# One Trainium2 core, a hybrid encoder block: DMA scratch of 64 bytes, and the first two w_up jobs prepared between the last output tiles

## The chip, the cores and the metric

The kernel runs on one core of a Trainium2 chip, with five engines: TensorE (PE in the profile; PEld is its weight load), VectorE (DVE), ScalarE (ACT), GpSimd (POOL) and SyncE (SP, which issues nearly all DMAs here). Each engine has a queue of its own that is worked off strictly in order; engines wait for each other by semaphores. The metric is the device time of one execution in microseconds. Everything is float32; products are made by splitting each operand into a high part (type fp32r) and the remainder, and multiplying hi*hi, hi*lo and lo*hi.

## The reference

What is computed, with one sequence of 1024 positions and a model width of 1024:

```
h  = rmsnorm(x, g_mix) * (1 + scale1) + shift1
proj = h @ w_in                      # q, k, v of two mixers, two gates
ya = dilated attention @ w_branch_dil;  yb = 2-D neighbourhood attention @ w_branch_na
merged = sigmoid(ga) * ya + sigmoid(gb) * yb
x  = x + gate1 * (merged @ w_out)
h2 = rmsnorm(x, g_ffn) * (1 + scale2) + shift2
u  = depthwise_conv3(h2 @ w_up)      # 2 * 2816 columns
x  = x + gate2 * ((gelu(u_gate) * u_val) @ w_down)
y  = rmsnorm(x, g_final)
```

The change lies at the border between `merged @ w_out` and `h2 @ w_up`.

## The kernel before

**Layout.** Activations are held transposed: 128 channels on the partitions, positions along the free axis, in two halves of 512 positions. A tile of 128x512 float32 takes 2 KB of each partition.

**Output tiles.** `out_tile(hf, m, ...)` makes 128 channels (m = 0 to 7) of one half (hf = 0, 1) of `merged @ w_out`: 24 matmuls (L77 to L79) over the merged tiles `mhi` and `mlo`, then the residual (DVE, L948), a store to scratch (L949, SP), the square (ACT, L954; DVE, L952, for m = 7), the scaling by `am2` (ACT, L955) and the running sum of squares (L957, on POOL, or on DVE for the second half with m over 2). The weights of the next tile are loaded into `wraw` (two buffers), split by ACT (L55, into `whi`) and POOL (L56, into `wlo`), with two buffers each, so a tile's weights can be split only when the products of the tile two before are done.

**The norm between.** After the last tile of a half, `add_sums` (L89, PE) adds the squares into `pcol`, `rstd_of` turns it into a factor `rs` (L94 DVE, L95 ACT, L96 DVE), `bcast` (L102, PE) spreads it over a PSUM bank `pbc`, and DVE multiplies the eight scaled tiles with it (L979 for the first half, L1078 for the second).

**The up products.** `h2 @ w_up` is done in 22 jobs of two 128-column blocks by a Strassen-Winograd scheme on 2x2 blocks: seven products instead of eight. The moving side's operands (B11, B21, T2, T1, T3, B22, T4) are sums and differences of the quarter blocks, made once: B11 and B21 from the first half's tiles `m1`, the rest from `m1` and the second half's tiles `m2`. In a block of fixed order (L1076 onward) DVE makes for k = 0 to 9 the scaling of `m2[k]` (L1078), `t2 = m2 + m1` (L1080), `m1 = m2 - t2` (L1082) and the low parts of T2 (L937) and T1 (L763); ACT the high parts (L936, L762); POOL `m1[4+k] - t2[k]` (L1089), and T3, B22 and T4 follow. Ahead of that `m2[0..3]` are replaced by differences to `m2[4..7]`: three by POOL (L991), the last by DVE (L997).

**The weights' side.** `a_operands` is a generator that prepares one job's weights in steps; each `next` emits one:

- setup, three POOL sums of 128x512: `S1 = a21 + a22` (L780), `S2 = S1 - a11` (L781), `a21 = a11 - a21` (L782);
- "row": ACT and DVE (for these two jobs) split a11 and a12 into `whi`, `wlo`;
- "sums": S2 and S1 are split into `wsh` (ACT) and `wsl` (POOL), then DVE makes `a12 - S2` (L789);
- "S3": a21 and a22 are split into another `wsh`, `wsl`;
- "S4": `a12` is split into a tile of the pool `big`.

`wsh` and `wsl` have three buffers each and lie in a pool `up` that is opened after the merged tiles' pool `mg` is released; part of it takes the addresses of `mhi` and `mlo`, so what is written there waits for the last output product. The pool `big` has nine buffers of 4 KB: four hold `m1`, two the raw weights of job 0 (`up_load`, L964), others the sums, S4, `t2` and the convolution's outputs. Job 1's raw weights take the two `wraw` buffers.

**Order.** Where no order is fixed, a planner puts each engine's instructions in order when the program is built: what is earlier in the program goes first, but an instruction whose inputs and buffers are there by the planner's clock may be put ahead of earlier ones that are not ready. On the chip the queues are then fixed. PE's order around the border is written out by hand from the last output tile on.

Of the kernel before, what the change touches and what calls it, by code (L numbers as in the profile page):

```python
# [9 lines left out]
FT = mybir.dt.float32  # L10
FR = mybir.dt.float32r
AF = mybir.ActivationFunctionType
OP = mybir.AluOpType
# [5 lines left out]
KT = 8  # L19
FF = 22  # L20
# [8 lines left out]
def hybrid_encoder(tc, xT, c, w_ada, small, w_in, w_v, p1_bias, p23_bias, na_bias, ln2_mult, ident, w_br, w_out,  # L29
                   w_up, w_down, out):  # L30
    nc = tc.nc
    act, dve, pool, pe, sp = nc.scalar, nc.vector, nc.gpsimd, nc.tensor, nc.sync

    const = tc.alloc_tile_pool(name="const", bufs=1)
    wpool = tc.alloc_tile_pool(name="w", bufs=2)
# [7 lines left out]
    sm = const.tile([128, 248], FT, name="sm")  # L43
# [3 lines left out]
    dve.memset(ones, 1.0)  # L47
    ada = const.tile([128, 48], FT, name="ada")
    am1 = const.tile([128, KT], FT, name="am1")
    am2 = const.tile([128, KT], FT, name="am2")  # L50
    b_ada, g_mix, g_ffn, g_fin = sm[:, 0:48], sm[:, 48:56], sm[:, 56:64], sm[:, 64:72]
    conv = sm[:, 72:248].rearrange("p (j m) -> p j m", j=4)

    def split(raw, hi, lo, lo_eng):
        act.activation(hi, raw, AF.Copy)  # L55
        lo_eng.tensor_tensor(lo, raw, f(hi), OP.subtract)  # L56
# [33 lines left out]
                      stop=last and t == n - 1, skip_group_check=True)  # L90

    def rstd_of(pcol, n):
        r = wpool.tile([128, KT], FT, name="rs", bufs=2)
        dve.tensor_scalar(r[:, :n], pcol[:, :n], 1.0 / D, EPS, OP.mult, OP.add)  # L94
        act.activation(r[:, :n], r[:, :n], AF.Sqrt)  # L95
        dve.reciprocal(r[:, :n], r[:, :n])  # L96
        return r
# [162 lines left out]
    with tc.manual_schedule(engines={e.engine for e in (sp, act, dve, pool, pe)}):  # L260
# [17 lines left out]
        r = rstd_of(pcol, 4)  # L278
# [26 lines left out]
        r = rstd_of(pcol, 4)  # L305
# [5 lines left out]
        for n in range(24):  # L311
            g, k = divmod(n, 8)
# [15 lines left out]
            i = n // 2 - 2  # L328
# [4 lines left out]
            if n % 2 and n >= 9:  # L333
                i = (n - 9) // 2
# [400 lines left out]
    with tc.tile_pool(name="gate", bufs=1, reuse_waits="tile") as work:  # L735
# [3 lines left out]
        for m in range(KT):  # L739
# [3 lines left out]
            for hf in range(2):  # L743
                sg = []
                for br in range(2):
# [3 lines left out]
                    p = ps.tile([128, 512], FT, name="pj", bufs=6)  # L749
# [19 lines left out]
    def a_operands(raw, n, work, st, lo_eng=pool, last=False):  # L769
# [12 lines left out]
        pool.tensor_tensor(a21, a11, a21, OP.subtract)  # L782
        hi, lo = (wpool.tile([128, KT, 128], FR, name=t).rearrange("p (a b) m -> p a b m", a=2)[:, :, :n]
                  for t in ("whi", "wlo"))
        pair(raw[0], ("11", "12"), hi, lo, lo_eng)
        yield
        hi, lo = (work(t).tile([128, 2, n, 128], FR, name=t, bufs=3) for t in ("wsh", "wsl"))
        pair(ws, ("S2", "S1"), hi, lo)
        dve.tensor_tensor(a12, a12, S2, OP.subtract)  # L789
        yield  # L790
        hi, lo = (work(t).tile([128, 2, n, 128], FR, name=t, bufs=3) for t in ("wsh", "wsl"))
        pair(raw[1], ("S3", "22"), hi, lo)
        yield
        s4 = work("wsl").tile([128, 2, n, 128], FR, name="wsl", bufs=3) if last else big([128, 2, n, 128], FR)
        pair(raw[0][:, 1:2], ("S4",), s4[:, 0:1], s4[:, 1:2])
        yield

    def products(st, n, moving, done, seq=range(7), in_psum=False):

# [127 lines left out]
    oppools = [tc.alloc_tile_pool(name=n, bufs=1, reuse_waits="tile") for n in ("B11", "B21")]  # L927
# [32 lines left out]
    def up_load(t):  # L960
        raw = []
        for i in range(2):
            r = big([128, KT, 128]) if t in (0,) or t > 1 and t % 2 else wpool.tile([128, KT, 128], FT, name="wraw")
            sp.dma_start(r, w_up[t + FF * i])  # L964
            raw.append(r.rearrange("p (a b) m -> p a b m", a=2))
        return raw

    raw = [big([128, 2, 512]) for _ in range(4)]
# [9 lines left out]
    for k in range(KT):  # L978
        dve.tensor_tensor(m1[k], m1[k], bc, OP.mult)  # L979
# [4 lines left out]
    sqa = wide()  # L984
    for m in range(KT - 1):
        m2.append(half_tile())
        out_tile(1, m, sqa, m2[m])
        if m == 3:
            raw = {0: up_load(0)}
        if m > 3:  # L990
            pool.tensor_tensor(m2[m - 4], m2[m], m2[m - 4], OP.subtract)  # L991
    sts = [{} for _ in range(FF)]
# [4 lines left out]
    dve.tensor_tensor(m2[3], m2[7], m2[3], OP.subtract)  # L997
# [6 lines left out]
    with tc.tile_pool(name="up", bufs=2, reuse_waits="tile") as work:  # L1004
        def conv_in(y, t, hf, src):
            act.activation(y[:, halves[hf]], src, AF.Identity, bias=conv[:, 3, t:t + 1], scale=conv[:, 1, t:t + 1])  # L1006

# [45 lines left out]
        def advance(g):  # L1053
# [20 lines left out]
        with tc.manual_schedule(engines={act.engine, dve.engine, pool.engine}):  # L1074

            for k in range(10):  # L1076
                if k < 8:
                    dve.tensor_tensor(m2[k], m2[k], bc, OP.mult)  # L1078
                if 1 <= k < 5:
                    dve.tensor_tensor(t2[k - 1], m2[k - 1], m1[k - 1], OP.add)  # L1080
                elif k >= 5 and k < 9:
                    dve.tensor_tensor(m1[k - 5], m2[k - 1], t2[k - 5], OP.subtract)  # L1082
                if 2 <= k < 6:
                    t_split("T2", k - 2, t2[k - 2], shift2[:, 2 + k:3 + k])
                elif k >= 6:
                    operand(m1[k - 6], ops["T1"][0][:, k - 6], ops["T1"][1][:, k - 6], dve)
            for k in range(4):
                t_split("T3", k, m2[k], dshift[:, k:k + 1])
                pool.tensor_tensor(m1[4 + k], m1[4 + k], t2[k], OP.subtract)  # L1089
            for k in range(4):  # L1090
                late["B22"].append((half_tile(FR), half_tile(FR)))
                shifted(m2[4 + k], shift2[:, 4 + k:5 + k], *late["B22"][k])
            for k in range(4):
                late["T4"].append((half_tile(FR), half_tile(FR)))
                operand(m1[4 + k], *late["T4"][k], pool)
# [3 lines left out]
        for t in range(FF):  # L1099
# [8 lines left out]
            for j in gens[t] if t < 2 else up_products(t, sts[t]):  # L1108
# [7 lines left out]
                if t == FF - 1 and j == 3:  # L1116
# [6 lines left out]
    for p in oppools[::-1]:  # L1123
        p.release()

    x3 = {}
# [10 lines left out]
    sts = [{} for _ in jobs]  # L1137
# [189 lines left out]
```

## Time and profile before

| | |
|---|---|
| three runs | 1591.77 us median, 1590.76 to 1592.05 |
| profiled execution | span 1588.7 us from first to last instruction; its own time outside the span is not recorded |
| PE busy | 1513.5 us (95%) |
| DVE, ACT, POOL busy | 1058.9, 804.8, 741.8 us |
| last output tiles of the second half | about 864 to 903 us |
| norm, T operands, first two up jobs | about 903 to 973 us |

Start times are microseconds from the span's start. A timeline row gives start, duration, engine, line, operation, output and inputs, the count of merged instructions, and in brackets the engine's idle time before the row and what ended it. Several merged instructions share one row, and the duration is then that of the row. A row of the waits gives who waited for whom, the total, the number of times and the longest. A row of a table by stage gives the stage, its length, each engine's busy time with its count of instructions, then the granted clock, the share of the DMA engines and GB/s.

### The profile page before, as it was taken

To read this page: it belongs to the slowest core of one execution; us is meant where nothing else is said; L and a number is where in the kernel's file an instruction comes from. 1 tells how busy PE (TensorE), PEld (TensorE's weight loads), DVE (VectorE), ACT (ScalarE), POOL (GpSimd) and SP (SyncE) were. 2 spreads that over 40 slices of the span, in tenths; PEclk is the share of its full clock that TensorE was granted. 3 is DMA by queue.
4 is the path that set the end of the run, shared out by engine and by line. 5 is a ranking of instruction groups with operands and counts; after the bars stand their busy time and mean duration, and the time that the engine had idled before them with its cause. 6 is when DMAs were issued, how large, how long until landed. Compare 5 with 4: busy or idle time off the path is not lost.

```text
span 1588.7 us, 21184 instructions
## 1 busy us (share of the span) xinstructions
PE 1513.5 (95%) x7582; PEld 1273.0 (80%) x7582; DVE 1058.9 (67%) x1905; ACT 804.8 (51%) x1451; POOL 741.8 (47%) x475
## 2 busy tenths in 40 slices
PE   8998999999998999999899889999999999999998
PEld 7787888888887988888678777788888887778787
DVE  7694457676667666535532898876666667787765
ACT  3420666675756766634334445444444446475542
POOL 2310423432214433411236768676666665588621
PEclk8999999999999999999999999999999999999999
DMA  9477522322223443546544312222222223433313
GB/s 376 185 287 264 140 72 72 101 68 79 67 76 112 140 107 105 173 129 209 159 144 154 113 53 80 80 95 92 80 80 80 80 82 137 153 128 131 113 54 106
DMA packets 107442, 196.81 MB, mean 124 GB/s; under 512 B 39845, under 2 KB 55077, under 8 KB 107301
## 3 DMA queue, kind: packets, MB, share of 16 engines
q1 hardware_dynamic: 107064, 195.20, 37.3%
q8 instruction: 59, 0.97, 0.3%
q14 instruction: 47, 0.38, 0.1%
q10 hardware_dynamic: 272, 0.26, 0.1%
HBM read 158.73 MB, written 42.47 MB: 127 GB/s over the span
## 4 chain that ended last, share of the span: by engine, by line
PE 63%; DVE 14%; DMA 6%; ACT 6%; POOL 5%; issue 5%; SPq 1%; DVEq 0%; ACTq 0%; POOLq 0%
PE pj L817 9%; PE pj L816 9%; PE pj L818 9%; PE pj L77 8%; PE pj L79 8%; PE pj L78 8%; DVE mt L151 2%; DMA g<-gs 2%; DVE big L1012 2%; PE pj L378 2%; ACT ks L403 2%; DMA wraw<-w_down 2%; PE O L666 1%; POOL wlo L56 1%; DVE kl L405 1%
## 5 line engine op out<-in xcount | busy, mean ns | idle before, releaser
L56 POOL TENSOR_TENSOR wlo<-wraw,whi 128x1024 fp32r<-128x1024 f32 (+1 forms) x77 | 179.8, 2336 | 289.9 <-ACT whi L55 277.9
L77 PE MATMUL pj<-h,whi 128*128 128x512 f32 x448 | 179.9, 402 | 8.9 <-DVE kl L405 7.0
L78 PE MATMUL pj<-h,whi 128*128 128x512 f32 x448 | 178.4, 398 | 0.0
L79 PE MATMUL pj<-h,wlo 128*128 128x512 f32 x448 | 178.1, 398 | 0.0
L56 POOL TENSOR_TENSOR wsl<-big,wsh 128x1024 fp32r<-128x1024 f32 (+1 forms) x45 | 109.4, 2432 | 50.2 <-ACT wsh L55 50.1
L1012 DVE SCALAR_TENSOR_TENSOR big<-wc,sm,big 128x256 f32<-128x256 f32 (+1 forms) x132 | 117.0, 934 | 17.3 <-ACT big L1006 17.2
L55 ACT ACTIVATE whi<-wraw 128x1024 fp32r<-128x1024 f32 (+1 forms) x79 | 80.7, 1021 | 83.3 <-POOL wc L957 20.3
L77 PEld LDWEIGHTS pj<-h,whi 128*128 128x128 f32 x448 | 85.0, 190 | 25.6 <-issue 5.1
L79 PEld LDWEIGHTS pj<-h,wlo 128*128 128x128 f32 x448 | 84.8, 189 | 15.7
L78 PEld LDWEIGHTS pj<-h,whi 128*128 128x128 f32 x448 | 85.2, 190 | 15.0
L491 DVE CUSTOM_DVE_ANT_0 P<-S,bias 128x256 f32<-128x256 f32 x128 | 52.3, 421 | 55.5 <-PE S L538 40.2
L405 DVE SCALAR_TENSOR_TENSOR kl<-pj,ks 64x512 fp32r<-64x512 f32 x64 | 56.5, 883 | 43.8 <-ACT ks L403 40.0
L443 POOL TENSOR_TENSOR vv<-vv 96x256 fp32r<-96x256 f32 (+2 forms) x32 | 40.9, 1286 | 95.6 <-ACT vv L442 79.4
L492 ACT ACTIVATE P<-P,st 128x256 f32<-128x256 f32 x128 | 64.3, 503 | 39.7 <-DVE st L491 39.2
L1012 DVE SCALAR_TENSOR_TENSOR big<-pj,sm,big 128x512 f32<-128x512 f32 x132 | 67.9, 565 | 16.1 <-ACT big L1006 16.1
L385 POOL TENSOR_SCALAR qb<-qs 128x256 fp32r<-128x256 f32 x32 | 26.4, 851 | 105.9 <-DVE qs L369 51.1
L1006 ACT ACTIVATE big<-wc,sm 128x512 f32<-128x512 f32 x44 | 35.8, 816 | 76.6 <-DVE wc L829 46.0
L644 POOL TENSOR_SCALAR P<-P,stb 128x288 f32<-128x288 f32 (+1 forms) x32 | 40.4, 1263 | 66.1 <-DVE stb L641 60.4
L56 POOL TENSOR_TENSOR wsl<-wraw,wsh 128x768 fp32r<-128x768 f32 (+1 forms) x23 | 49.9, 2169 | 43.3 <-ACT wsh L55 39.1
L403 ACT ACTIVATE ks<-pj 64x512 fp32r<-64x512 f32 x64 | 53.7, 838 | 21.1 <-DVE kl L405 10.0
L1038 ACT ACTIVATE big<-big 128x1024 f32<-128x1024 f32 x22 | 23.3, 1060 | 79.7 <-DVE big L1012 79.7
L55 ACT ACTIVATE wsh<-big 128x1024 fp32r<-128x1024 f32 (+1 forms) x45 | 44.8, 999 | 36.4 <-POOL big L781 21.9
(366 smaller groups left out, 4864.8 us busy)
## 6 DMA issues: line engine op xcount, KB each, us to landing
wraw<-w_in SPq DMA_DIRECT2D x32, 512.0 KB, 3.8
t<-w_ada SPq DMA_DIRECT2D x24, 512.0 KB, 7.8
big<-w_up SPq DMA_DIRECT2D x22, 512.0 KB, 5.2
wraw<-w_up SPq DMA_DIRECT2D x22, 512.0 KB, 3.5
as<-big SPq DMA_DIRECT2D x22, 512.0 KB, 2.6
big<-as SPq DMA_DIRECT2D x22, 512.0 KB, 6.1
wraw<-w_down SPq DMA_DIRECT2D x24, 384.0 KB, 3.8
x<-w_ada SPq DMA_DIRECT2D x16, 512.0 KB, 8.9
```

What stands on the lines that cost most here:

```text
L55: act.activation(hi, raw, AF.Copy)
L56: lo_eng.tensor_tensor(lo, raw, f(hi), OP.subtract)
L77: pe.matmul(psum, whi[:, k0 + k], mhi, start=k == 0, stop=False)
L78: pe.matmul(psum, whi[:, k0 + k], mlo, start=False, stop=False)
L79: pe.matmul(psum, wlo[:, k0 + k], mhi, start=False, stop=k == n - 1)
L403: act.activation(kh[x], pp[a], AF.Copy, scale=0.125)
L405: dve.scalar_tensor_tensor(ll[x], pp[a], 0.125, f(kh[a]), OP.mult, OP.subtract)
L492: act.activation(pp, pp, AF.Exp, bias=mi, scale=-1.0, accum_out=li)
L816: pe.matmul(psum, whi[:, k], bhi, start=j < 4 and k == 0, stop=False, skip_group_check=True)
L817: pe.matmul(psum, whi[:, k], blo, start=False, stop=False, skip_group_check=True)
L818: pe.matmul(psum, wlo[:, k], bhi, start=False, stop=k == n - 1, skip_group_check=True)
L1012: dve.scalar_tensor_tensor(y[:, dst], src, wt, y[:, dst], OP.mult, OP.add)
```

## The change

- The reservation for DMA descriptors at the bottom of each partition shrinks to 64 bytes. `am2` moves into the first eight columns of `sm` (the first biases of `b_ada`), and `rs` has one buffer instead of two.
- The pool `up` is opened before the second half's output tiles and no longer shares addresses with `mhi`, `mlo`.
- Both jobs' raw weights go into `big`; they are loaded at tiles m = 1 and m = 3 in program order (before: job 0's at m = 3, job 1's after the tiles).
- With `order` given, setup is a step of its own. Tiles 2, 3 and 4 emit job 0's setup, "sums" and "S3"; tiles 5 and 6 job 1's setup and "sums". After the tiles come job 0's "row", job 1's "row", job 0's "S4". `a12 - S2` comes after "row" instead of after "sums". Job 1's "S3" and "S4" stay in job 0's products.
- The DVE subtraction for `m2[3]` (L997) moves from ahead of the norm's sums into the fixed block, at k = 2.

```
-        r = wpool.tile([128, KT], FT, name="rs", bufs=2)
+        r = wpool.tile([128, KT], FT, name="rs", bufs=1)
...
-    am2 = const.tile([128, KT], FT, name="am2")
+    am2 = sm[:, 0:8]
...
+        steps = order or ("row", "sums", "S3", "S4")
+        if order:
+            yield
+        for step in steps:
...
+            if step == ("row" if order else "sums"):
+                dve.tensor_tensor(a12, a12, S2, OP.subtract)
+            yield
...
-            r = big([128, KT, 128]) if t in (0,) or t > 1 and t % 2 else wpool.tile([128, KT, 128], FT, name="wraw")
+            r = big([128, KT, 128]) if t < 2 or t % 2 else wpool.tile([128, KT, 128], FT, name="wraw")
...
+    work = tc.alloc_tile_pool(name="up", bufs=2, reuse_waits="tile")
+    prep = []
     for m in range(KT - 1):
         m2.append(half_tile())
         out_tile(1, m, sqa, m2[m])
-        if m == 3:
-            raw = {0: up_load(0)}
+        if m in (1, 3):
+            t = m // 2
+            prep.append(a_operands(up_load(t), 4, lambda t: work, sts[t], dve,
+                                   order=("sums", *(("S3", "row") if t == 0 else ("row", "S3")), "S4")))
+        if m > 1:
+            next(prep[m > 4])
...
-    dve.tensor_tensor(m2[3], m2[7], m2[3], OP.subtract)
...
-        raw[1] = up_load(1)
-        prep = [a_operands(raw.pop(t), 4, lambda t: work, sts[t], dve) for t in range(2)]
-        next(prep[0])
-        next(prep[1])
-        for _ in range(3):
-            next(prep[0])
-        next(prep[1])
+        raw = {}
+        for i in (0, 1, 0):
+            next(prep[i])
...
             for k in range(10):
+                if k == 2:
+                    dve.tensor_tensor(m2[3], m2[7], m2[3], OP.subtract)
...
-    nc = bacc.Bacc("TRN2", target_bir_lowering=False, num_devices=1)
+    nc = bacc.Bacc("TRN2", target_bir_lowering=False, num_devices=1, dynamic_dma_scratch_size=64)
```

More of the change, by code (lines that the diff above doesn't have):

```diff
@@ L767, in hybrid_encoder, with a_operands @@
     names = tuple(b for _, b in STEPS)
-    def a_operands(raw, n, work, st, lo_eng=pool, last=False):
+    def a_operands(raw, n, work, st, lo_eng=pool, last=False, order=None):
         a11, a12, a21, a22 = raw[0][:, 0], raw[0][:, 1], raw[1][:, 0], raw[1][:, 1]
@@ L782, in a_operands, with two @@
         pool.tensor_tensor(a21, a11, a21, OP.subtract)
[L783 to L796, printed above, removed]
+        def two(src, names):
+            hi, lo = (work(t).tile([128, 2, n, 128], FR, name=t, bufs=3) for t in ("wsh", "wsl"))
+            pair(src, names, hi, lo)
+        steps = order or ("row", "sums", "S3", "S4")
+        if order:
+            yield
+        for step in steps:
+            if step == "row":
+                hi, lo = (wpool.tile([128, KT, 128], FR, name=t).rearrange("p (a b) m -> p a b m", a=2)[:, :, :n]
+                          for t in ("whi", "wlo"))
+                pair(raw[0], ("11", "12"), hi, lo, lo_eng)
+            elif step == "sums":
+                two(ws, ("S2", "S1"))
+            elif step == "S3":
+                two(raw[1], ("S3", "22"))
+            else:
+                s4 = work("wsl").tile([128, 2, n, 128], FR, name="wsl", bufs=3) if last else big([128, 2, n, 128], FR)
+                pair(raw[0][:, 1:2], ("S4",), s4[:, 0:1], s4[:, 1:2])
+            if step == ("row" if order else "sums"):
+                dve.tensor_tensor(a12, a12, S2, OP.subtract)
+            yield
     def products(st, n, moving, done, seq=range(7), in_psum=False):
@@ L984, in hybrid_encoder @@
     sqa = wide()
+    sts = [{} for _ in range(FF)]
+    work = tc.alloc_tile_pool(name="up", bufs=2, reuse_waits="tile")
+    prep = []
     for m in range(KT - 1):
@@ L987, in hybrid_encoder @@
         out_tile(1, m, sqa, m2[m])
-        if m == 3:
-            raw = {0: up_load(0)}
+        if m in (1, 3):
[4 more added lines that the diff above has]
+            next(prep[m > 4])
         if m > 3:
             pool.tensor_tensor(m2[m - 4], m2[m], m2[m - 4], OP.subtract)
-    sts = [{} for _ in range(FF)]
     late_mm = contextlib.ExitStack()
@@ L1002, in hybrid_encoder @@
     late = {n: [] for n in ("B22", "T4")}
-    with tc.tile_pool(name="up", bufs=2, reuse_waits="tile") as work:
+    if True:
         def conv_in(y, t, hf, src):
@@ L1122, in hybrid_encoder @@
                         next(more)
-    for p in oppools[::-1]:
+    for p in (work, *oppools[::-1]):
         p.release()
```

## The prediction

> **What bounds the kernel now.** I read the page first, then the table by stage, then who PE waits for, then each queue's timeline around the border.
>
> ```profile
> span 1588.7 us, 21184 instructions
> ```
> ```profile
> 1000.00:1350.00 350.00, 348.62 (x1532) 286.85 (x1530) 246.51 (x358) 161.86 (x207) 232.28 (x130) 1.00 0.27 91
> ```
> ```profile
> 864.00:885.00 21.00, 21.00 (x96) 17.23 (x95) 16.12 (x20) 12.78 (x19) 10.48 (x7) 1.00 0.35 110
> 885.00:905.00 20.00, 19.71 (x90) 16.02 (x89) 15.19 (x11) 8.91 (x13) 15.81 (x9) 1.00 0.44 149
> ...
> 913.00:927.00 14.00, 12.13 (x46) 9.38 (x44) 14.00 (x15) 5.20 (x8) 12.62 (x7) 0.88 0.00 1
> 927.00:936.00 9.00, 6.11 (x25) 4.60 (x26) 9.00 (x13) 5.95 (x10) 2.90 (x1) 1.00 0.18 58
> ```
>
> From 1000 to 1350 us PE is busy 348.62 of 350 us (0.228 us a matmul), so what the border gains arrives later undiminished. The output tiles (864 to 905) are PE-bound too. In the two stretches from 913 to 936 it is DVE that has no idle time: 14.00 of 14 and 9.00 of 9. PE's waits of 855 to 945, and then of 945 to 1000, say on what it depends:
>
> ```profile
> PE pbc L102 <- DVE rs L96: 4.1, 1, 4.1
> PE pj L817 <- DVE T1lo L763: 2.4, 1, 2.4
> PE pj L817 <- DVE T2lo L937: 2.4, 1, 2.4
> PE pj L79 <- POOL wlo L56: 0.3, 1, 0.3
> ```
> ```profile
> PE pj L816 <- ACT wc L822: 2.7, 1, 2.7
> PE pj L816 <- DVE wc L826: 1.9, 1, 1.9
> ```
>
> That is 8.9 us at the border and 4.6 behind it. DVE's queue ahead of the first wait, and ACT's step in it:
>
> ```profile
> 905.31 2.27 DVE L56 TENSOR_TENSOR wlo<-wraw,whi 128x1024 fp32r<-128x1024 f32 x1
> 907.67 1.60 DVE L789 TENSOR_TENSOR wraw<-wraw,big 128x512 f32<-128x512 f32 x1
> 909.20 0.15 DVE L94 TENSOR_SCALAR rs<-pcol 128x4 f32<-128x4 f32 x1
> 909.27 2.75 DVE L997 TENSOR_TENSOR x<-x,x 128x512 f32<-128x512 f32 x1
> 911.94 0.17 DVE L96 RECIPROCAL rs<-rs 128x4 f32<-128x4 f32 x1
> 912.91 1.29 DVE L1078 TENSOR_TENSOR x<-x,pbc 128x512 f32<-128x512 f32 x2 [0.81 <-PE pbc L102]
> ```
> ```profile
> 905.18 2.94 ACT L55 ACTIVATE wsh<-big 128x1024 fp32r<-128x1024 f32 x3
> ...
> 909.38 0.21 ACT L95 ACTIVATE rs<-rs 128x4 f32<-128x4 f32 x1 [0.65 <-DVE rs L94]
> ```
>
> The factor `rs` waits behind job 1's row split, its `a12 - S2` and the subtraction for `m2[3]`. These are long because POOL works beside them:
>
> ```profile
> 863.01 1.29 POOL L782 TENSOR_TENSOR big<-big 128x512 f32<-128x512 f32 x1
> ...
> 908.68 8.37 POOL L56 TENSOR_TENSOR wsl<-big,wsh 128x1024 fp32r<-128x1024 f32 x3
> ```
>
> Job 0's sums were ready at 864.3 (863.01 + 1.29), but their split starts at 905.18, when the last output product is done: the shared addresses hold it back 41 us, and three `wsl` then occupy POOL until 917.05, into the T operands.
>
> **The change part by part.**
>
> ```profile
> 899.03 1.23 DVE L56 TENSOR_TENSOR wlo<-big,whi 128x1024 fp32r<-128x1024 f32 x1 [0.16 <-DMA wraw<-w_up]
> ...
> 927.35 0.68 DVE L1078 TENSOR_TENSOR x<-x,pbc 128x512 f32<-128x512 f32 x1
> 927.95 0.68 DVE L1082 TENSOR_TENSOR big<-x,big 128x512 f32<-128x512 f32 x1
> ```
> ```profile
> 912.25 0.62 PE L102 MATMUL pbc<-idt,rs 128*128 128x128 f32 x4 [4.09 <-DVE rs L96]
> ...
> 935.06 0.50 PE L817 MATMUL pj<-T1lo,wsh 128*128 128x512 f32 x1 [2.41 <-DVE T1lo L763]
> ```
>
> *The wait for rs.* Moving L997 behind the broadcast takes out what lies between ACT's root (done at 909.59) and L96 (911.94): 2.3 us. The row split and L789 stay ahead of L94: the row's buffers come free only when the last output tile ends, as now. But beside a quiet POOL they would take 1.23 and 0.68 instead of 2.27 and 1.60: 2.0 us less. POOL isn't surely quiet then, for job 0's S4 is still split on it there. Bounds: 2.3 with POOL as busy as now, 4.1 where PE no longer waits. I take **3.5**, as the three `wsl` (8.37 us) are gone and one split stays.
>
> The clock of 0.88 in the 14 us behind this wait costs 1.7 us of PE time. It brings nothing of its own, since PE then waits for T2 and T1 anyway; it does show that 4.09 us of idle time slow PE, while after the T1lo wait of 2.4 the clock is 1.00 (927 to 936).
>
> *The T operands.* From 912.91 to the last T1lo (PE goes on at 935.06) DVE takes 22.15 us for 26 operations: eight scalings, four sums, four differences, eight low parts, two evacuations. Back to back without POOL they start 0.60 apart (927.35, 927.95): 15.6 us. The other 6.5 come with some 15.5 us of POOL work (12.62 and 2.90 in the two stretches): 0.42 us per us. The change takes away POOL's `wsl` up to 917.05, 4.1 us: **1.7** gained (bounds 0, if job 2's work moves up in its place, and 3.7, at the 0.9 per us found below). It adds L997: **0.6** lost (bounds 0.6 and 2.75). Net 1.1. The queue behind T1lo is DVE work again, so the shift passes through.
>
> *What moves into the output tiles.* Three ACT splits (2.94 us together) and three `wsl` of POOL, 7.2 us at 2.40 each; job 1's setup comes a little earlier. POOL is busy 10.48 + 15.81 of the 41 us, so 14.7 are idle. There is room, but the output weights pass through the same queue:
>
> ```profile
> 868.46 4.87 DVE L979 TENSOR_TENSOR big<-big,pbc 128x512 f32<-128x512 f32 x8 [3.58 <-PE pbc L102]
> ...
> 873.91 3.79 DVE L937 SCALAR_TENSOR_TENSOR B11lo<-big,ada,B11hi 128x512 fp32r<-128x512 f32 x4
> 877.63 4.22 DVE L937 SCALAR_TENSOR_TENSOR B21lo<-big,ada,B21hi 128x512 fp32r<-128x512 f32 x3
> ...
> 885.36 2.41 DVE L957 TENSOR_TENSOR wc<-wc 128x512 f32<-128x512 f32 x1 [1.53 <-ACT wc L954]
> ```
> ```profile
> 882.54 0.63 ACT L954 ACTIVATE wc<-x 128x512 f32<-128x512 f32 x1 [5.20 <-DVE x L948]
> ...
> 883.69 1.04 ACT L55 ACTIVATE whi<-wraw 128x1024 fp32r<-128x1024 f32 x1
> ```
> ```profile
> 871.04 2.42 POOL L56 TENSOR_TENSOR wlo<-wraw,whi 128x1024 fp32r<-128x1024 f32 x1 [3.54 <-ACT whi L55]
> 875.85 1.30 POOL L957 TENSOR_TENSOR wc<-wc 128x512 f32<-128x512 f32 x1 [2.40 <-ACT wc L954]
> ...
> 883.31 1.30 POOL L957 TENSOR_TENSOR wc<-wc 128x512 f32<-128x512 f32 x1 [3.34 <-ACT wc L954]
> 884.81 2.41 POOL L56 TENSOR_TENSOR wlo<-wraw,whi 128x1024 fp32r<-128x1024 f32 x1 [0.20 <-ACT whi L55]
> ...
> 893.59 2.40 POOL L56 TENSOR_TENSOR wlo<-wraw,whi 128x1024 fp32r<-128x1024 f32 x1 [1.09 <-ACT whi L55]
> ```
> ```profile
> 887.27 0.50 PE L79 MATMUL pj<-mhi,wlo 128*128 128x512 f32 x1 [0.29 <-POOL wlo L56]
> ```
>
> The last `wlo` (893.59) ends at 896.0, and its tile begins at about 897.9 (887.0 plus two tiles of 24 matmuls): 1.9 us to spare. A `wsl` of 2.40 that has just started ahead of it makes it 0.5 late. Bounds: nothing, and the 7.5 of the slow rival below. I take **0.5** lost, one such collision.
>
> *Loads.* Job 1's two loads leave `wraw` and go ahead on SP's queue, past loads of w_out and stores of x:
>
> ```profile
> big<-w_up SPq DMA_DIRECT2D x4, 512.0 KB, 5.6
> ```
>
> The DMA engines are 0.35 to 0.44 busy there, and a w_out load has a whole tile of 5.5 us to land, so I put this at nothing; without that cover it is 5.6, one landing, at one tile. Job 2's loads can start once `wraw` is free of the last output weights, ahead of need: nothing gained. *Nothing* also for the smaller scratch (the page's DMA queues are hardware and instruction queues, none fed by POOL), for `am2` (its columns' last reader is long done) and for the single `rs` (one norm is in work at a time). The price of the `big` pool is not in the trace: job 1's raw weights hold two of nine buffers until its S3 and S4 are split. I put it at nothing, because the outputs that need `big` next come when `t2` and `m1` give theirs back; bounds 0 and 2.7, one PE wait like the longest behind the border.
>
> *Sum:* 3.5 + 1.1 - 0.5 = **4.1 us** faster. The span would be 1584.6 instead of 1588.7. The median of the runs shown is 3.1 above this span, which I keep: 1591.77 - 4.1 = **1587.7**.
>
> **The rivals.**
>
> *The output weights come late (slower).* DVE's backlog of B11lo and B21lo (873.91 to 881.85) holds up the residual; ACT's L954 waits for that (5.20 idle), and `whi` stands behind L954 in ACT's queue; so `wlo` came just too late at 887.27 already. The backlog's seven operations took 7.9 us instead of 4.2 (at 0.60), with 4.1 us of POOL work beside them: 0.9 us per us. POOL is idle there for 1.9 (until 875.85) and 1.9 us (from 879.97). If hoisted splits fill these, `whi` comes 3.8 x 0.9 = 3.4 later; a `wsl` in front of `wlo` adds 2.4; over 4 us of idle PE then brings the slow clock, 1.7. Together 7.5, less 4.6 from the other terms: 2.9 slower, **1594.7**. It decides from 4.6 us of added PE wait on. For it: no reserve at 887. Against it: of POOL's 10.5 us of idle time in 864 to 885 only these 3.8 lie beside the backlog; 2.6 lie beside L979, which reads PSUM and went at 0.61 each though a `wlo` (871.04) ran beside it.
> The Trainium skill (SBUF — State Buffer, "Who interferes with whom") speaks for this rival: a DVE instruction with two SBUF inputs and a GpSimd instruction that reads SBUF exclude each other, and whichever issues second stands until the first is through. By that rule, the trace agrees: L957 of 885.36 ended 0.55 us after the `wlo` that had started at 884.81. By the rule the price is 1.0 us per us of POOL instead of 0.9, and the rival would come out 0.4 us later.
>
> *rs stays late.* The planner's order is open: it may leave POOL's overhang (a late `wsl`, S4's split, L991) beside the row split and L789. The same follows if the buffers aren't really clear. Then L997's 2.3 - 0.6 stays, less 0.5: 1.2 faster, **1590.6**. Job 2's setup, moved up into the T operands, would take another 3 x 1.29 x 0.42 = 1.6. For it: POOL's 33.5 us of work in 41 don't fall evenly, and three of five preparing steps are emitted at tiles 4 to 6, whose stretch has 4.2 us idle.
>
> *The later waits go too.* The waits of 2.7 and 1.9 follow from ACT and DVE catching up; with work moved ahead of the border they may vanish: 4.1 + 4.6 = 8.7, **1583.1**. Against it: jobs 1 and 2 pass through the same three `wsh` buffers as before.
>
> **How the numbers follow.** Forecast 0.45, with a range of its own from 1585.5 to 1589.5; late output weights 0.12; rs late 0.23; later waits gone 0.20. What differs by less than 0.2% (3.2 us) can't be told from no change. Faster: 0.20 and 0.37 of the forecast's 0.45 = 0.57. Slower: most of the slow rival, 0.11. Same: the rest, 0.32. The range leaves out the worse half of the slow rival, collisions at several tiles, and what goes beyond the last rival: 1582.5 to 1594.0.
>
> **What would show it.** Right: `wsh` splits start before 900; L96 at about 908.5; no PE wait for rs over 1 us; clock 1.00 in 913 to 927; T2lo and T1lo waits of about 2 us still there; the last output product ending at about 904. Wrong: PE waits on `wlo` of over 1 us in the output tiles, POOL busy on `wsl` behind the broadcast, or new waits between 935 and 1000 for tiles of `big`.

## The result: slower, and the profile after

The changed kernel takes **1601.36 us** (median of 4 runs, 1598.9 to 1604.03) against 1591.26 for the kernel before on the same chip: ratio **1.0064**, 95% interval 1.0049 to 1.0079. Run again on another chip it gave 1.0041 (1.0016 to 1.0065). The forecast was 1587.7, with a range of 1582.5 to 1594.0: the time lies outside it, and on the slower side. The profiled execution took 1601.83 with a span of 1600.0, 11.3 us longer than before's 1588.7.

In the changed kernel the lines are numbered differently: the residual is L956, the square L962, the running sum L965, the low part of B L945, `a12 - S2` L803, the scaling L1089, the subtraction for `m2[3]` L1087, and the up products L824 to L826. First PE's waits from 855 to 945, then from 945 to 1012:

```profile
PE pj L77 <- ACT whi L55: 7.6, 1, 7.6
PE pj L825 <- DVE T2lo L945: 2.9, 2, 1.8
PE pj L79 <- POOL wlo L56: 0.9, 1, 0.9
...
PE pj L824 <- DVE wc L834: 3.3, 1, 3.3
PE pj L824 <- ACT wc L830: 2.5, 1, 2.5
```

The wait for `rs` (4.1) and the one for `T1lo` (2.4) are gone, as forecast. One new wait of 7.6 us for output weights stands in their place. DVE's queue from the low parts of B to the norm's end:

```profile
877.21 6.51 DVE L945 SCALAR_TENSOR_TENSOR B11lo<-big,ada,B11hi 128x512 fp32r<-128x512 f32 x4
883.65 6.95 DVE L945 SCALAR_TENSOR_TENSOR B21lo<-big,ada,B21hi 128x512 fp32r<-128x512 f32 x4
890.52 1.40 DVE L956 SCALAR_TENSOR_TENSOR x<-pj,ada,x 128x512 f32<-128x512 f32 x2
...
917.42 0.75 DVE L956 SCALAR_TENSOR_TENSOR x<-pj,ada,x 128x512 f32<-128x512 f32 x1 [1.15 <-PE pj L79]
...
921.10 0.18 DVE L96 RECIPROCAL rs<-rs 128x4 f32<-128x4 f32 x1 [0.27 <-ACT rs L95]
922.45 1.28 DVE L1089 TENSOR_TENSOR x<-x,pbc 128x512 f32<-128x512 f32 x2 [1.17 <-PE pbc L102]
...
924.25 0.69 DVE L1087 TENSOR_TENSOR x<-x,x 128x512 f32<-128x512 f32 x1
```

The four B11lo take 6.51 us instead of 3.79. POOL beside them has no gap:

```profile
874.38 1.28 POOL L780 TENSOR_TENSOR big<-big 128x512 f32<-128x512 f32 x1
875.64 2.41 POOL L56 TENSOR_TENSOR wlo<-wraw,whi 128x1024 fp32r<-128x1024 f32 x1
878.01 1.74 POOL L781 TENSOR_TENSOR big<-big 128x512 f32<-128x512 f32 x1
879.71 1.76 POOL L782 TENSOR_TENSOR big<-big 128x512 f32<-128x512 f32 x1
881.42 1.75 POOL L965 TENSOR_TENSOR wc<-wc 128x512 f32<-128x512 f32 x1
883.14 2.84 POOL L56 TENSOR_TENSOR wsl<-big,wsh 128x1024 fp32r<-128x1024 f32 x1
885.94 2.79 POOL L56 TENSOR_TENSOR wlo<-wraw,whi 128x1024 fp32r<-128x1024 f32 x1
```

L780 to L782 and the `wsl` of 883.14 are job 1's setup and sums. The residual, late by them, holds ACT's square, and `whi` is queued behind the square; PE stands until `whi` comes, and goes on at a lower granted clock, 0.54 and then 0.78 in the stages of 5 us (ACT's timeline, PE's timeline, then the table by stage):

```profile
891.29 0.63 ACT L962 ACTIVATE wc<-x 128x512 f32<-128x512 f32 x1 [9.50 <-DVE x L956]
...
892.44 1.04 ACT L55 ACTIVATE whi<-wraw 128x1024 fp32r<-128x1024 f32 x1
```
```profile
885.53 0.39 PE L78 MATMUL pj<-mlo,whi 128*128 128x512 f32 x1
893.53 0.80 PE L77 MATMUL pj<-mhi,whi 128*128 128x512 f32 x1 [7.62 <-ACT whi L55]
894.13 0.63 PE L78 MATMUL pj<-mlo,whi 128*128 128x512 f32 x1
```
```profile
890.00:895.00 5.00, 1.47 (x4) 1.18 (x5) 2.81 (x4) 3.32 (x5) 2.71 (x2) 0.54 0.51 175
895.00:900.00 5.00, 5.00 (x19) 3.97 (x18) 1.48 (x1) 0.00 (x0) 0.93 (x1) 0.78 0.40 140
```

The two profiled executions compared by marks that both have (start times, us):

| stretch | before | after | difference |
|---|---|---|---|
| start to the first half's L94 | 862.86 | 865.86 | +3.0 |
| to the last residual of the output tiles | 40.76 | 51.56 | +10.8 |
| to the first scaling behind `rs` | 9.29 | 5.03 | -4.3 |
| to the first store of an up job | 50.88 | 49.99 | -0.9 |
| to the last such store | 394.71 | 397.70 | +3.0 |
| to the end | 230.20 | 229.86 | -0.3 |

The "first half's L94" is the start of that half's norm; the residuals behind it are those of the second half's output tiles. The 10.8 us there are, row by row: 7.6 of waiting for `whi`, 0.6 more of waiting for `wlo` (0.9 instead of 0.3), 1.7 by the slower clock behind the wait (from 893.53 to 897.12 eight matmuls started 0.45 us apart instead of 0.2334), and 0.6 by a wider spacing of the 192 matmuls (0.0033 us each, explained below).

### The profile page after: what moved, and what is told of

Its sections match the earlier page's. It is cut to its first block, busy times and chain, and to the rows that moved or that the text cites. A ratio compares the mean times of both kernels' runs of the same rounds, so it can differ in the third digit from the quotient of the medians.

```text
span 1600.0 us, 21188 instructions
## 1 busy us (share of the span) xinstructions
PE 1522.4 (95%) x7582; PEld 1272.6 (80%) x7582; DVE 1052.0 (66%) x1905; ACT 806.2 (50%) x1451; POOL 738.4 (46%) x475
## 4 chain that ended last, share of the span: by engine, by line
PE 63%; DVE 12%; DMA 7%; POOL 6%; ACT 6%; issue 5%; SPq 1%; DVEq 0%; ACTq 0%; POOLq 0%
PE pj L77 8%; PE pj L79 8%; PE pj L824 8%; PE pj L825 8%; PE pj L78 8%; PE pj L826 8%; DMA g<-gs 2%; PE pj L378 2%; DVE big L1025 2%; DMA wraw<-w_down 2%; POOL wsl L56 2%; DVE mt L151 2%; PE O L666 2%; ACT ks L403 1%; ACT whi L55 1%
## 5 line engine op out<-in xcount | busy, mean ns | idle before, releaser
L77 PE MATMUL pj<-h,whi 128*128 128x512 f32 x448 | 182.0, 406 | 8.5 <-DVE kl L405 6.6
L78 PE MATMUL pj<-h,whi 128*128 128x512 f32 x448 | 180.8, 404 | 0.0
```

The source lines that it names most:

```text
L77: pe.matmul(psum, whi[:, k0 + k], mhi, start=k == 0, stop=False)
L78: pe.matmul(psum, whi[:, k0 + k], mlo, start=False, stop=False)
```

## The experiments

Each ratio is to runs of the kernel before on the same chip.

**The moved POOL work, taken out of the way.** Job 1's setup and sums are queued behind the third tile's running sum:

```
+            marks[hf, m] = (dve if hf and m > 2 else pool).tensor_tensor(sqa, sqa, sq, OP.add)
...
         if m > 1:
-            next(prep[m > 4])
+            with tc.issue_after(marks[1, 2].ins) if m > 4 else contextlib.nullcontext():
+                next(prep[m > 4])
```

> The changed kernel, with job 1's setup and sums queued on POOL behind the third tile's running sum, so that they cannot run beside B11lo and B21lo on DVE. Theory A (POOL's work beside DVE's backlog delays the residual, ACT's square behind it and the next weights): the eight low parts take at most 9 us instead of 13.4, the PE wait of 7.6 on whi is gone, about 1592. Theory B (the backlog does not matter, the planner's order on PE does): the backlog still takes about 13, and the time falls only as PE's order happens to change.

Measured: **0.9981** (0.9961 to 1.0001). The wait for `whi` is gone, and the eight low parts are back to 8.6 us in all, from 13.4:

```profile
873.90 3.77 DVE L945 SCALAR_TENSOR_TENSOR B11lo<-big,ada,B11hi 128x512 fp32r<-128x512 f32 x4
877.60 4.87 DVE L945 SCALAR_TENSOR_TENSOR B21lo<-big,ada,B21hi 128x512 fp32r<-128x512 f32 x4
```

The output tiles take 43.98 us instead of 51.56. So 7.6 of the 10.8 us come from where this POOL work lies. (With this edit the planner also keeps PE's matmuls in the order of the tiles; what that order does is taken apart next.) Of the 3.2 us that stay, 2.0 are waits for `wlo` (2.3 instead of 0.3) and 0.6 the wider spacing.

**PE's own order.** In the changed kernel the planner put two matmuls of the sixth output tile, which need the late `whi`, ahead of the fifth tile's; PE stood for them from 885.92 with 22 of the fifth tile's matmuls queued behind, although that tile's `wlo` was done at 888.73 (885.94 + 2.79). This edit keeps the order of the program on PE; all other queues are the same:

```
+    pe_order = contextlib.ExitStack()
+    pe_order.enter_context(tc.manual_schedule(engines={pe.engine}))
     for m in range(KT - 1):
...
+    pe_order.close()
```

> The changed kernel with PE's order fixed tile by tile in the second half's output tiles; every other queue is the same, and of PE's only two matmuls of the sixth tile move, which the planner had put ahead of the fifth tile's first product with wlo. If these two matter (PE stands for the sixth tile's whi with a whole tile of work behind it), the wait of 7.6 turns into about 3 for the fifth tile's wlo and 1 for the sixth's, about 1597. If only the late whi matters, the time stays at 1601 within 1.

Measured: 0.9998 (0.9981 to 1.0016). The low parts are as stretched as with the change (13.7 us), but PE's waits in the output tiles are these:

```profile
PE pj L79 <- POOL wlo L56: 4.0, 2, 2.8
PE pj L825 <- DVE T2lo L945: 3.2, 2, 1.8
```

The tiles take 48.28 us: the order on PE accounts for 3.3 of the 10.8. The other way round, with PE's order left and ACT's and POOL's tails of the third and fourth tile queued behind the sixth tile's weights (`last_split` holds the two instructions that split them, `tail` the square, the scaling and the running sum):

```
+        if hf and m == 4:
+            with tc.issue_after(last_split[0].ins), tc.issue_after(last_split[1].ins):
+                for t in tails:
+                    t()
...
+        if hf and m in (2, 3):
+            return tails.append(tail)
```

> The changed kernel, with the squares and scalings of the third and fourth tile queued behind the sixth tile's weight split, on ACT and POOL; PE's order stays as in the changed kernel. Theory A (whi stands behind the late square in ACT's queue): whi is split about 886, the PE wait falls from 7.6 to about 3 (until the fifth tile's wlo), about 1596. If the wait has another cause, a late load of weights for one, it stays at 7.6 and the time at 1601.

Measured: 0.9998 (0.9980 to 1.0017); PE's wait for `whi` is 0.5 us, and the tiles take 47.17. Both links of the chain (square ahead of `whi`, two matmuls out of turn) were needed for the 7.6. By their ratios both runs are back at the time of before, which is more than the 3.3 and 4.4 us of the tiles; against the 1.0041 of the changed kernel's second series the intervals allow that, and against the 1.0064 of the first the rest isn't explained.

**The price by itself.** Three extra POOL instructions on a tile that nobody else reads, in the kernel before with the new addresses, at the place where POOL was idle beside the low parts (`low[0]` is the low part of the fourth tile's weights):

```
         out_tile(1, m, sqa, m2[m])
+        if m == 2:
+            with tc.issue_after(low[0].ins):
+                for _ in range(3):
+                    pool.tensor_tensor(d[:, 1024:1536], d[:, 0:512], d[:, 512:1024], OP.add)
```

> A price by itself: the kernel before with the smaller scratch and the clear addresses (e1_layout), with three extra POOL additions of 128x512 (1.3 us each, two SBUF inputs, on a tile nobody else reads) queued behind the low part of the fourth tile's output weights, where POOL is idle beside DVE's low parts B11lo and B21lo. If each us of POOL beside them costs DVE 0.9 to 1.0 us: the seven low parts take 10.5 to 11.3 us instead of 7.85, the third tile's residual starts 3 us later (relative to the first low part), and PE waits 2 to 3 us for output weights where it waited for nothing. If the stretching in the changed kernel had another cause (the split of wsl, its DMA loads): 7.9 us as now.

In the second kernel that line is `pool.memset(d[:, 1024:2048], 0.0)`.

> As e8_tt, but the three extra POOL instructions are memsets of 128x1024 that read no SBUF and write to a tile nobody else uses. If what stretches DVE's low parts is POOL's reading of SBUF: the seven low parts take 7.9 us as without them (plus at most 0.9 us per us by which the running sum and the weights' low part are pushed into other places). If any POOL work does it: 10 us or more, as with the additions (10.52).

One profile each. DVE and POOL with the additions, then with the memsets (L939 and L950 are L937 and L948 of before):

```profile
873.96 6.49 DVE L939 SCALAR_TENSOR_TENSOR B11lo<-big,ada,B11hi 128x512 fp32r<-128x512 f32 x4
880.38 4.19 DVE L939 SCALAR_TENSOR_TENSOR B21lo<-big,ada,B21hi 128x512 fp32r<-128x512 f32 x3
884.48 0.74 DVE L950 SCALAR_TENSOR_TENSOR x<-pj,ada,x 128x512 f32<-128x512 f32 x1
```
```profile
873.47 3.02 POOL L996 TENSOR_TENSOR pad<-pad 128x512 f32<-128x512 f32 x2
```
```profile
873.37 2.74 DVE L939 SCALAR_TENSOR_TENSOR B11lo<-big,ada,B11hi 128x512 fp32r<-128x512 f32 x4
876.02 5.26 DVE L939 SCALAR_TENSOR_TENSOR B21lo<-big,ada,B21hi 128x512 fp32r<-128x512 f32 x3
881.20 0.74 DVE L950 SCALAR_TENSOR_TENSOR x<-pj,ada,x 128x512 f32<-128x512 f32 x1
```
```profile
872.86 3.00 POOL L996 MEMSET pad<- 128x1024 f32 x3
875.83 1.44 POOL L959 TENSOR_TENSOR wc<-wc 128x512 f32<-128x512 f32 x1
877.22 2.85 POOL L56 TENSOR_TENSOR wlo<-wraw,whi 128x1024 fp32r<-128x1024 f32 x1
```

With the additions the seven low parts take 10.52 us, and PE waits 2.3 us for `wlo`, where it waited for nothing. With the memsets they take 7.83, as without any extra work (7.85): the four B11lo started 0.66 us apart beside them, and what stretches B21lo is the running sum and the weights' low part that come then. It is POOL's reading of SBUF that costs, not its being busy. The Trainium skill (SBUF — State Buffer, "Who interferes with whom") says so: a DVE instruction with two SBUF inputs contends with a GpSimd instruction that reads SBUF, and not with one that only writes it.

**The subtraction for `m2[3]` alone.** Before, with L997 moved to k = 2 of the fixed block:

```
-    dve.tensor_tensor(m2[3], m2[7], m2[3], OP.subtract)
...
+                if k == 2:
+                    dve.tensor_tensor(m2[3], m2[7], m2[3], OP.subtract)
```

> Before with one edit: the subtraction for m2[3] moves from ahead of the norm's factor into the fixed block at k = 2. By the working of the prediction: 2.3 us off the wait for rs (4.1 to about 1.8), 0.6 added to the T operands, 1.7 us faster (ratio 0.9989). Rival: PE's gain at rs is given back at the T operands, whose eight scalings can start only when PE's spread factor is there and which DVE then works off without a gap, with the moved subtraction now among them: T2lo and T1lo waits grow by what rs loses, ratio 1.000.

Measured: 0.9996 (0.9976 to 1.0015). PE's waits and the moved instruction:

```profile
PE pj L817 <- DVE T2lo L937: 5.8, 4, 2.4
PE pbc L102 <- DVE rs L96: 1.8, 1, 1.8
```
```profile
911.07 2.90 DVE L1077 TENSOR_TENSOR x<-x,x 128x512 f32<-128x512 f32 x1
```

The wait for `rs` shrinks from 4.1 to 1.8, exactly as worked out: the first scaling comes 6.99 us after the last residual instead of 9.29. All of it is given back by the first store of a job, 53.52 us later instead of 50.88: beside the `wsl`, the moved subtraction takes 2.90 us in DVE's unbroken queue, where the changed kernel has 0.69. The rival had the outcome right, and only part of the place: PE waits 5.8 us for T2lo where T2lo and T1lo together made 4.8, and the slow stretch of its clock, in before behind the wait for `rs` (0.88 in 913 to 927), comes later and is longer (0.81 in 920 to 925, 0.50 in 925 to 930). In this profile the step pays nothing without the quiet POOL; the ratio by itself can't tell, for its interval holds the 0.9989 of the working as well as 1.

**The addresses alone.** Before, with the scratch of 64 bytes, `am2` and `rs` as in the change, and an unused tile that keeps `up` nearly where it was; the order up to the border is that of before:

```
+    with tc.tile_pool(name="pad", bufs=1, reuse_waits="tile") as pad, \
+            tc.tile_pool(name="up", bufs=2, reuse_waits="tile") as work:
+        reserve(pad, (("pad", 16320, 1),))
```

> The kernel before with the new layout only: DMA scratch of 64 bytes, am2 in sm, one rs, and an unused pool of 16,320 bytes ahead of `up`, so that `up` lies over the merged tiles as before. Each engine's order up to the border is that of the kernel before. If the shifted addresses cost time by themselves (the 4.8 us that the changed kernel lost before 225 us, and the 0.1 us a job between 1100 and 1330), this takes 1594 to 1598. If the early loss is chance of the clock gate or hangs on the order of work, it takes 1591.3, within 1.

Measured: 1.0011 (0.9991 to 1.0032), not to be told from no change. But the profile shows an effect that I had missed. Between 1100 and 1300 us PE is never idle, so the count of matmuls there gives their spacing. The rows of before, of the changed kernel and of this one:

```profile
1100.00:1300.00 200.00, 200.00 (x881) 165.20 (x880) 135.18 (x200) 86.51 (x103) 131.49 (x73) 1.00 0.24 82
```
```profile
1100.00:1300.00 200.00, 200.00 (x876) 164.22 (x876) 132.80 (x198) 87.98 (x105) 133.82 (x76) 1.00 0.24 83
```
```profile
1100.00:1300.00 200.00, 200.00 (x872) 163.35 (x871) 134.22 (x199) 86.01 (x102) 129.58 (x72) 1.00 0.24 81
```

An up job of 84 matmuls takes 19.09, 19.19 and 19.30 us in every profile of each layout (median from store to store). Sorted by operands, with the address of the weights less that of the moving operand, modulo 512 bytes (the addresses are those of the built programs; starts over 0.3 us apart, where a record is missing, are left out):

```
mean start-to-start, us (1100 to 1300)   before          after           addresses alone
B11, B21 with whi, wlo                   -64: 0.2290     -32: 0.2327     -32: 0.2326
T, x with wsh, wsl                         0: 0.2266       0: 0.2270     -64: 0.2293
x with big (S4)                            0: 0.2267       0: 0.2267       0: 0.2266
```

So the spacing follows the distance, not the operands. Test: reserve the 32 bytes of `rs` at the front of the pool `w`; this moves only the weights' buffers, by 32 bytes, to distance 0, and every queue stays as it was.

```
     wpool = tc.alloc_tile_pool(name="w", bufs=2)
+    wpool.tile([128, KT], FT, name="rs", bufs=1)
```

> The changed kernel with one line more: the 32 bytes of rs are reserved at the front of the pool `w` instead of at its end. All queues are the same; only wraw, whi and wlo move, by 32 bytes, so that the weights' addresses and the moving operands' agree modulo 512 bytes (before: 64 bytes short of it; with the change: 32 short). Theory: matmul spacing depends on that distance, as the three layouts run so far suggest (distance 0: 0.2267 us in the T and x products; 64 short: 0.2289 for B11hi,whi of before; 32 short: about 0.2330 for the same in the changed kernel). Then an up job takes 84 x 0.2267 = 19.04 us instead of 19.19, 22 jobs bring 3.3, and the 768 products of the gated branches and the output tiles with the 216 of the down products some 6 more: 8 to 10 us faster than the changed kernel, 1590 to 1593 where before has 1591.5. Rival: the job time of 19.19 belongs to the order of the queues and not to the addresses: 19.19 again, 1599.

In the kernel before, whose `rs` has two buffers, the same line with `bufs=2` moves them by 64 bytes.

> The same line in the kernel before (64 bytes there, for two buffers of rs): the weights' distance goes from 64 short to 0. By the theory of the addresses: an up job 19.04 instead of 19.08 us, 0.9 us over 22 jobs, and 0.003 to 0.004 us on each of about 1000 products of branches, output tiles and down: 4 to 5 us faster in all, ratio 0.997. By the rival: 1.000.

Measured: the changed kernel with it **1.0004** (0.9991 to 1.0018), against 1.0041 and 1.0064 without; the kernel before with it **0.9969** (0.9950 to 0.9987). In both, an up job takes 19.03 us, and all products are 0.2267 apart. The row of the changed kernel with it:

```profile
1100.00:1300.00 200.00, 200.00 (x884) 165.68 (x883) 136.58 (x205) 87.36 (x105) 133.16 (x74) 1.00 0.23 79
```

Its wait for `whi` is as long as ever (7.8 us), so the late weights don't come from the addresses.

**The changed kernel once more.**

> The changed kernel once more, in more executions. If the loss is in the program (POOL's moved work beside DVE's B11lo and B21lo, then the PE order with two matmuls of the sixth tile ahead of the fifth tile's): PE again waits over 5 us for `whi` in the output tiles, the four B11lo take about 6.5 us instead of 3.8, and the ratio is 1.005 to 1.007 (8 to 11 us). If half of the 10 us was the early loss around 170 us (first store of the gates at 224.6 instead of 219.8), which I take to depend on the single execution: that store is back at 219 to 221 in this profile, and the ratio is 1.002 to 1.004 (3 to 6 us).

Measured: 1.0041 (1.0016 to 1.0065). The 7.6 us for `whi` are there again, the four B11lo take 6.54 us, the tiles 51.88. The first store of the gates is at 221.85 instead of 224.58 (before: 219.82). In the first profile PE had fallen to half clock at 175, in this one not (the rows of before, of the changed kernel, and of this execution):

```profile
175.00:180.00 5.00, 5.00 (x27) 4.22 (x26) 2.60 (x4) 3.86 (x9) 5.00 (x5) 1.00 0.69 174
```
```profile
175.00:180.00 5.00, 5.00 (x13) 3.85 (x13) 1.98 (x5) 4.14 (x9) 5.00 (x5) 0.50 0.66 178
```
```profile
175.00:180.00 5.00, 4.97 (x21) 4.04 (x22) 2.06 (x6) 4.60 (x10) 5.00 (x6) 1.00 0.70 179
```

So most of that early loss belongs to the single execution, and not to the change. The four other profiles with the changed kernel's addresses, and its queues up to 874 us, have that store at 218.80 to 221.12.

**A version that beats both.** To the kernel with job 1's POOL work later, one more instruction is moved. There POOL split the low part of job 2's row (2.82 us) in the middle of the T operands, and one T2lo took 2.85 us beside it. The changed kernel has the same (the last two rows are its own):

```profile
919.89 2.82 POOL L56 TENSOR_TENSOR wlo<-wraw,whi 128x1024 fp32r<-128x1024 f32 x1
```
```profile
920.40 2.85 DVE L945 SCALAR_TENSOR_TENSOR T2lo<-wc,ada,T2hi 128x512 fp32r<-128x512 f32 x1
```
```profile
925.00:930.00 5.00, 4.33 (x10) 3.46 (x11) 5.00 (x8) 2.40 (x4) 1.69 (x1) 0.50 0.00 0
```
```profile
930.80 2.83 POOL L56 TENSOR_TENSOR wlo<-wraw,whi 128x1024 fp32r<-128x1024 f32 x1
```
```profile
931.31 2.86 DVE L945 SCALAR_TENSOR_TENSOR T2lo<-wc,ada,T2hi 128x512 fp32r<-128x512 f32 x1
```

This edit moves that split:

```
-                next(nxt)
+                with tc.issue_after(marks["t"].ins) if t == 1 else contextlib.nullcontext():
+                    next(nxt)
```

(`marks["t"]` is the last low part of T4.)

> The kernel with job 1's POOL work behind the third tile's running sum (e2_job1_later), and one POOL instruction moved: the low part of job 2's row, which there ran from 919.89 for 2.82 us beside a T2lo of 2.85 us (the others 0.74), goes behind the four low parts of T4. If POOL work beside DVE's two-input operations is what makes the T operands late: that T2lo takes about 0.7 again, the T2lo waits of 1.8 and 1.4 shrink below 1.0 each, the clock of 0.50 in 925 to 930 goes, and the kernel is 2 to 3.5 us faster than e2_job1_later (first store of an up job at 958 to 960 instead of 961.7; ratio to before about 0.996). Rival: the next operand, T1lo, takes the wait over, or job 2 wants its row early: within 1 us of e2_job1_later.

Measured: **0.9966** (0.9946 to 0.9987). The third T2lo is back at 0.74, PE's waits are 1.4 us (T2lo) and 1.1 us (T1lo), the half clock is gone, and the first store of an up job comes at 959.63 instead of 961.70, 47.27 us behind the first scaling instead of 50.15:

```profile
921.22 0.74 DVE L945 SCALAR_TENSOR_TENSOR T2lo<-wc,ada,T2hi 128x512 fp32r<-128x512 f32 x1
```
```profile
925.00:930.00 5.00, 4.69 (x20) 3.26 (x18) 5.00 (x8) 2.13 (x4) 1.69 (x1) 1.00 0.00 0
```

With the line for `rs` as well:

> The same line in e7_row2_later (job 1's POOL work later, job 2's row behind T4), which took 1586.9 there against 1591.5 before. By the theory of the addresses: up job 19.04 us, 8 to 10 us less, ratio to before 0.990 to 0.992. By the rival: 0.9966 again.

Measured: **0.9921** (0.9892 to 0.9950), median 1579.78 against 1593.66. The two gains add up within the intervals.

## Why the prediction was wrong, point by point

**The wait for `rs` (3.5 gained): right.** From the last residual to the first scaling the changed kernel takes 5.03 us instead of 9.29: 4.3, a little over the upper bound of 4.1. POOL was quiet there, and L803 and the row split ran short (0.69 and 1.22 us for the last of them). What the step didn't say is that the 2.3 of L997 bring nothing without that quiet (the profile of the experiment with it alone).

**The T operands (1.7 gained, 0.6 lost): right in the number, in part by luck.** L997, now L1087, takes 0.69. The stretch from the first scaling to the first store of a job is 0.9 shorter, against the 1.1 forecast. But two larger things nearly cancel in it. Without the `wsl` the early T operands run short (the first T2lo takes 0.74 instead of 1.78); and job 2's row split, which before ran beside T1lo, now runs beside a T2lo (2.86). With it the long wait moved: the one for T1lo went, those for T2lo stayed, at 2.9 in all, and the granted clock behind them is 0.50:

```profile
931.56 2.90 POOL L56 TENSOR_TENSOR wlo<-wraw,whi 128x1024 fp32r<-128x1024 f32 x1 [4.68 <-ACT whi L55]
```
```profile
935.00:940.00 5.00, 3.89 (x10) 2.75 (x9) 5.00 (x8) 2.22 (x4) 1.33 (x2) 0.50 0.00 0
```

(The first row is of before, the second of the changed kernel.) With that one split out of the way the stretch is another 2.9 shorter (50.15 to 47.27, in the version that beats both).

**What moves into the output tiles ("I take 0.5 lost, one such collision"): this step failed.** It lost 10.8 us. The mechanism was written down as the rival "The output weights come late", and place, chain and slow clock came out as there; what failed is the choice between the bounds, and the size of the upper one. Three things were missed:

- The rival's price was capped by the idle time that POOL had beside the backlog in the trace of before: 3.8 us. That is no cap. Each POOL operation that reads SBUF lengthens the backlog, and the longer backlog takes in more of POOL's queue, whose operations are lengthened too (L781 1.74 us; with DVE reading PSUM, setup took 1.28). POOL was busy without a gap for 11.5 us of the 13.4, where it had worked 3.9 beside the seven operations. The residual came 13.3 us after the first low part instead of 7.9: 5.4 late, not 3.4, of which 0.7 is the eighth low part, which before stood behind the residual. The price for each us of POOL was about right. A low part by itself takes 0.66 (as beside the memsets; the prediction took the 0.60 of simpler operations), so POOL's work stretched the eight by 8.0 us. At the lengths that it has where DVE reads PSUM (1.28 for a 128x512 sum, 2.41 for a split) that work is 9.5 us: 0.84 per us. Before's seven, reckoned alike, were stretched by 3.2 for 3.7 us of POOL (the prediction's 4.1 count a gap of 0.3), 0.87 per us. By the rule of the Trainium skill that the prediction cites (the same section) it would be 1.0; the trace stays a little below it. It was the amount of POOL work beside the backlog that the prediction had too small.
- PE's order in the output tiles was taken as it was. The planner's order changed with the rest, and cost 3.3. Without it (the run with PE's order kept) the tiles lose 7.5.
- "It decides from 4.6 us of added PE wait on": 7.6 came. It had a chance of 0.12, argued down because only 3.8 of POOL's idle time lay beside the backlog; that argument rested on the first point.

**"Nothing also for the smaller scratch": wrong, by a smaller sum.** The weights' buffers moved by 16,352 bytes (the scratch and `am2`), the operands behind `rs` by 16,384, so `whi` and `wlo` came from 64 to 32 bytes short of the moving operands (modulo 512). In the up jobs this is 0.11 us each, 2 of the 3.0 us lost between first and last store. From 715 to 905 the products of `whi` and `wlo` are 0.2334 instead of 0.2301 apart (means over some 700), 2.5 us on 768 products if PE alone set the pace there. The input projections also use `whi` and `wlo` and aren't in this count: the median spacing of their products went from 0.229 to 0.232, but the time to the first half's L94 shows no loss with the addresses alone (860.66 against 862.86). The ratios say less: the addresses alone make 1.7 us, and the realignment brought the changed kernel 5.9 (1.0041 to 1.0004, on different chips) and the kernel before 5.0, a difference of 0.9; both are within their intervals of nothing. So some 1 to 4.5 us of the loss, an estimate from these rows and ratios that no run settles closer.

**Loads, `am2`, the single `rs`, `big`: no sign of a cost.** No new wait names a load. Behind the border the waits of 2.7 and 1.9 became 2.5 and 3.3: the rival "The later waits go too" fell, and the 1.2 more is not explained.

**Signs.** Right: `wsh` splits before 900, no wait for `rs` over 1 us, T2lo's waits. Wrong: L96 at 921.10 instead of 908.5, and the last output product late. The sign I had named for the failure was PE waiting for `wlo`; it waited for `whi`, one step earlier in the same chain. The clock is 1.00 behind the broadcast (920 to 930), but the slow stretch only moved on, behind the T2lo waits (0.50 in 935 to 940). So it took less idle time than the 4 us that the prediction reckoned with: the wait ahead of it was one of 1.8 us.

**Open.** The 3.0 us up to the first half's L94 came back to 1.6 in the second execution (864.43). Among the profiles with before's order that mark lies between 859.60 and 862.86, and in the four other profiles with the changed kernel's addresses and early queues between 860.92 and 863.33. So most of the 3.0 is probably chance of the single execution. One of the 3.0 us between the stores isn't placed either; with the same addresses that stretch is 396.4 in three other profiles and 397.8 in two.

## What to carry to other kernels

Idle time of an engine in the trace of before is no upper bound on what work moved beside a contended stretch will cost, since the stretch grows and draws in more of that engine's queue; lay the moved work where the other engine reads PSUM or is idle, and look at every queue that the planner rewrites, PE's among them. A price that is "nothing" because bytes only move is worth a row: compare the spacing of matmuls in a stretch without waits, and, where it costs nothing, keep weights and moving operands at the same offset modulo 512 bytes, as in the fastest layout run here. A step that takes work off one wait pays only if its new place is quiet.

## What the runs showed of the hardware

- Matmuls of 128x512 in back-to-back products started 0.2267 us apart where weights and moving operand lay at the same offset modulo 512 bytes, 0.2290 to 0.2293 where the weights lay 64 bytes short of it, and 0.2326 to 0.2327 at 32 bytes short. In all layouts run the moving operand lay at 480 modulo 512, so whether the distance counts or the weights' own offset stays open; the offsets were 480, 416 and 448, so modulo 64 alone would not tell the first two apart.
- POOL's memsets (3.00 us for three) left DVE's two-input operations alone (B11lo x4 2.74), and its additions did not (6.49).
- Behind a PE wait of 1.8 us that ended at 923.3, with one of 1.4 us to follow, the granted clock was 0.50 in 925 to 930; with a single 1.4 there, and T1lo waits of 1.1 together behind it, it was 1.00. In before two waits of 2.4 us, 7.6 us apart, left it at 1.00 (925 to 945). So the length of a wait did not decide it alone.
